# One head's two LRU gates as columns of one weight, rounded parts and remainders stacked along K: two products for three, on one Trainium2 core

## The chip, the core and the metric

The kernel runs on 1 core of one Trainium2 chip. The metric is device time in microseconds (us) of one launch. One core has a TensorE (PE in the profile; PEld is its weight load), a VectorE (DVE), a ScalarE (ACT), a GpSimd (POOL) and a SyncE (SP), which issues the DMAs here. Each takes its instructions in the order in which they were written into its queue.

## The reference

One decoder block over 2048 positions of 1024 channels, in fp32. The part that is changed is the gate of the linear recurrence, `rg_lru`; its 1024 channels are 16 heads of 64, and both gates are block diagonal: one 64x64 matrix per head.

```python
def block_diag_linear(x, w, b):
    xh = x.reshape(bt, s, LRU_HEADS, HEAD_DIM)
    y = jnp.einsum('bshi,hij->bshj', xh, w).reshape(bt, s, LRU_WIDTH)
    return y + b

def rg_lru(x, w_a, b_a, w_x, b_x, lam):
    r = jax.nn.sigmoid(block_diag_linear(x, w_a, b_a))
    i = jax.nn.sigmoid(block_diag_linear(x, w_x, b_x))
    log_a = -LRU_C * r * jax.nn.softplus(-lam)
    a = jnp.exp(log_a)
    bx = jnp.sqrt(-jnp.expm1(2.0 * log_a)) * (i * x)
    # h[t] = a[t] * h[t-1] + bx[t]
```

Around it: RMSNorm, one input projection (columns x and g of the recurrence, c, v and b of a short convolution), a causal convolution of 4 taps on x ahead of the gates, `gelu(g)` behind the recurrence, an output projection, and an MLP with squared ReLU.

## The kernel before

The sequence is cut into four blocks of 512 positions. Channels lie on the 128 partitions, positions along the free dimension. Every fp32 operand of a matmul is split into a part rounded to fp32r ("hi", made by ACT, L153) and a remainder ("lo", made by DVE, L154), and a product is taken as hi·hi + lo·hi + hi·lo (`passes`, L186).

For each block `mixers` (L933) runs four pairs of channel tiles. A pair is 256 channels, two tiles of 128, so four heads. For pair `pr` it runs, in program order, `lru_gelu` (48 matmuls into `ps_g`, then two ACT reads of that PSUM tile: a copy at L566 and a square at L567), `lru_conv` of the next pair (48 matmuls into `ps_x`, ACT copies them to `xr_in` at L536, DVE makes `xr` with 2 instructions at L541 and 6 at L550, then `xr_hi` and `xr_lo`), and `lru_scan` (L572: the gates into two PSUM tiles `psri`, two sigmoids of ACT each at L591 and L592, and then a chain of DVE and ACT instructions up to the scan at L610). After the fourth pair come the units of the short convolution: `ps_c`, `ps_v`, `ps_b`, twice. On PE the stage stands as ps_g, ps_x, psri, ps_g, ps_x, psri, ps_g, ps_x, psri, ps_g, ps_c, psri, ps_v, ps_b, and so on: the matmuls of the gates come one pair late.

PSUM is one pool of four tiles of two banks (L93), taken in turn in program order. In a pair these are ps_g, ps_x, psri, psri, so ps_g of a pair takes the tile of ps_g of the pair before, and the first ps_v takes that of the fourth ps_g. Its first matmul waits until ACT has read that tile for the second time (L567).

The weights of a unit are loaded two units ahead by SP and split by ACT and DVE (L144 to L184), through 15 slots. Temporaries go through 29 slots.

The gate weights are made at the start and again after the first MLP: for each of w_a and w_x a tile of 128 x 8 x 128 is set to zero by POOL (L267), the 64x64 blocks are loaded on its diagonal (L275), and it is split by ACT and POOL (L280). For the eight tiles of channels, both gates and three passes, that makes 6 matmuls per tile of channels and block.

Small parameters are loaded as 88 rows of `prow` (L310), turned by one transpose on PE (L454, `pps`) and copied by DVE to `prm` (L455). PE and DVE run that transpose and copy in the midst of the first projection, which is ordered by hand (L400).

Outside of two hand-ordered parts a planner orders the instructions of each engine's queue by its own estimate of when they can run, so the order on ACT and DVE can differ from block to block. The MLP (L675 to L872) isn't touched.

## Time and profile before

| what | value |
|---|---|
| median of 3 runs | 2218.67 us (2218.43 to 2218.98) |
| the profiled execution's own time | 2218.57 us |
| its span, first to last instruction | 2216.8 us |
| granted TensorE clock, mean of the span | 0.992 |
| PE, PEld busy | 98%, 81% |
| DVE, ACT, POOL busy | 1671.4 us (75%), 1039.1 us (47%), 62.2 us (3%) |
| matmuls, of these psri | 9684, 192 |

Busy time is summed over the span; the stages differ. A row of the timeline gives start, duration, engine, line, operation, output<-input, shapes, count, and in square brackets how long the engine was idle ahead of it and what ended that. The chain of waits follows the end of the program back through what released what; a row of it is start, duration, engine, tile and line.

### The profile page before, as it was taken

The page shows a single profiled execution, that of the slowest core. Times are in us where ns is not written, and L with a number is a line of the kernel's source. Part 1 is how long each engine was busy: PE and PEld are TensorE (multiplying, and loading weights), DVE is VectorE, ACT ScalarE, POOL GpSimd, SP SyncE. Part 2 cuts the span into 40 slices and gives each one's busy share as a digit, 9 for nine tenths or more (in the row PEclk, how much of TensorE's full clock was granted, in tenths as well). Part 3 has the DMA queues.
Part 4 walks back from the last instruction along what each step waited for, and adds up shares of the span by engine and source line. Part 5 has one row for each costly group of instructions (what it writes and reads, how often), then busy time and mean ns, then how long its engine had stood idle before and what let it go on. Part 6 is the DMA issues. An engine that isn't in the chain of part 4 may idle for free.

```text
span 2216.8 us, 25235 instructions
## 1 busy us (share of the span) xinstructions
PE 2176.6 (98%) x9684; PEld 1801.9 (81%) x9684; DVE 1671.4 (75%) x1948; ACT 1039.1 (47%) x1346; POOL 62.2 (3%) x62
## 2 busy tenths in 40 slices
PE   7999999999999999999999999999999999999997
PEld 6888888887888887888888888888888888788886
DVE  7887678868775767878888776886796665887767
ACT  4864478534332333334558644764443332433343
POOL 3010000000000000000100000010000000000000
PEclk8999999999999999999999999999999999999999
DMA  7334443432444386454172434234325345854432
GB/s 226 105 117 152 149 146 119 147 122 86 154 166 148 144 300 248 137 178 151 48 232 91 157 119 171 76 114 147 125 109 185 119 175 203 315 172 161 133 105 76
DMA packets 180776, 334.10 MB, mean 151 GB/s; under 512 B 14672, under 2 KB 106928, under 8 KB 180656
## 3 DMA queue, kind: packets, MB, share of 16 engines
q1 hardware_dynamic: 180656, 332.49, 43.7%
q8 instruction: 76, 1.25, 0.2%
q14 instruction: 44, 0.36, 0.1%
HBM read 252.76 MB, written 79.69 MB: 150 GB/s over the span
## 4 chain that ended last, share of the span: by engine, by line
PE 95%; DVE 4%; SPq 0%; DMA 0%; issue 0%; ACT 0%; DVEq 0%
PE dn L845 27%; PE up L731 26%; PE po L213 11%; PE ps_g L193 8%; PE ps_x L193 7%; PE ps_b L193 4%; PE ps_c L193 4%; PE ps_v L193 4%; PE psri L584 2%; DVE H L154 1%; PE start_x L420 1%; DVE w_lo L154 1%; PE tps L976 1%; DVE x L889 0%; DMA raw<-in_w_in_dram 0%
## 5 line engine op out<-in xcount | busy, mean ns | idle before, releaser
L731 PE MATMUL up<-H,w_hi 128*128 128x512 f32 x1792 | 553.7, 390 | 2.6 <-ACT w_hi L153 1.9
L731 PEld LDWEIGHTS up<-H,w_hi 128*128 128x128 f32 x1792 | 336.6, 188 | 73.5 <-ACT w_hi L153 2.7
L845 PE MATMUL dn<-w_lo,z_hi 128*128 128x512 f32 x896 | 350.2, 391 | 6.7 <-DVE w_lo L154 6.7
L731 PE MATMUL up<-H,w_lo 128*128 128x512 f32 x896 | 349.6, 390 | 3.2 <-DVE w_lo L154 3.2
L845 PE MATMUL dn<-w_hi,z_hi 128*128 128x512 f32 x896 | 349.8, 390 | 0.0
L845 PE MATMUL dn<-w_hi,z_lo 128*128 128x512 f32 x896 | 349.7, 390 | 0.0
L153 ACT CAST w_hi<-w 128x1024 fp32r<-128x1024 f32 x156 | 164.2, 1053 | 345.5 <-PE up L731 169.0
L154 DVE TENSOR_TENSOR w_lo<-w,w_hi 128x1024 fp32r<-128x1024 f32 x156 | 190.5, 1222 | 119.4 <-PE up L731 43.1
L154 DVE TENSOR_TENSOR w_lo<-raw,w_hi 128x1024 fp32r<-128x1024 f32 x156 | 191.6, 1231 | 99.4 <-ACT w_hi L153 45.5
L153 ACT CAST w_hi<-raw 128x1024 fp32r<-128x1024 f32 x160 | 165.6, 1047 | 104.0 <-PE po L213 68.0
L153 ACT CAST z_hi<-z 128x1024 fp32r<-128x1024 f32 x112 | 117.7, 1051 | 199.3 <-PE dn L845 160.9
L845 PEld LDWEIGHTS dn<-w_lo,z_hi 128*128 128x128 f32 x896 | 169.0, 189 | 42.6 <-DVE w_lo L154 7.6
L731 PEld LDWEIGHTS up<-H,w_lo 128*128 128x128 f32 x896 | 168.6, 188 | 39.8 <-DVE w_lo L154 4.9
L845 PEld LDWEIGHTS dn<-w_hi,z_hi 128*128 128x128 f32 x896 | 168.9, 189 | 35.4
L845 PEld LDWEIGHTS dn<-w_hi,z_lo 128*128 128x128 f32 x896 | 169.1, 189 | 35.0
L154 DVE TENSOR_TENSOR z_lo<-z,z_hi 128x1024 fp32r<-128x1024 f32 x112 | 138.3, 1235 | 59.3 <-issue 29.3
L857 DVE TENSOR_TENSOR x<-dn,x 128x1024 f32<-128x1024 f32 x112 | 136.4, 1220 | 23.5 <-PE dn L845 23.4
L213 PE MATMUL po<-w_hi,y_hi 128*128 128x512 f32 x384 | 119.4, 392 | 0.0
L213 PE MATMUL po<-w_hi,y_lo 128*128 128x512 f32 x384 | 118.3, 389 | 0.0
L213 PE MATMUL po<-w_lo,y_hi 128*128 128x512 f32 x384 | 118.3, 389 | 0.0
L193 PE MATMUL ps_g<-h_hi,w_hi 128*128 128x512 f32 x256 | 99.8, 390 | 0.0
L193 PE MATMUL ps_g<-h_lo,w_hi 128*128 128x512 f32 x256 | 99.6, 389 | 0.0
(222 smaller groups left out, 3571.4 us busy)
## 6 DMA issues: line engine op xcount, KB each, us to landing
raw<-in_w_in_dram SPq DMA_DIRECT2D x112, 512.0 KB, 3.6
z<-d_z SPq DMA_DIRECT2D x112, 512.0 KB, 4.2
w<-in_w_mlp_in_dram SPq DMA_DIRECT2D x64, 512.0 KB, 6.1
d_z<-snap SPq DMA_DIRECT2D x64, 512.0 KB, 3.5
raw<-in_w_out_dram SPq DMA_DIRECT2D x48, 512.0 KB, 3.7
d_z<-z SPq DMA_DIRECT2D x48, 512.0 KB, 2.9
w<-in_w_mlp_out_dram SPq DMA_DIRECT2D x48, 512.0 KB, 3.7
x<-in_x_dram SPq DMA_DIRECT2D x20, 512.0 KB, 8.5
```

The lines of the kernel that those rows point to most:

```text
L153: nc.scalar.copy(hi, src)
L154: (lo_engine or V).tensor_tensor(lo, src, hi.bitcast(F32), SUB)
L193: nc.tensor.matmul(ps[:, j, lo:hi], ws[k // 4][:, k % 4, j * P : (j + 1) * P], hs[:, k, lo:hi], start=k == 0 and i == 0, stop=k == KD - 1 ...
L213: nc.tensor.matmul(ps[:, half, :], ys[:, j, t * P : (t + 1) * P], ws[j][:, 0, half * 512 : (half + 1) * 512], start=first and i == 0, stop ...
L420: nc.tensor.matmul(start_x[:, j, 256 * th : 256 * th + 256], w[a][q][:, k, j * P : (j + 1) * P], h[b][:, 4 * q + k, 256 * th : 256 * th + ...
L584: nc.tensor.matmul(pr_[:, half, :], ws[:, c, :], xsrc[:, j, :], start=i == 0, stop=i == len(pl) - 1,)
L731: nc.tensor.matmul(ps[:, j, :], ws[:, k, j * P : (j + 1) * P], hs(k), start=i in (1, 2, 5) and k == 0 and n == 0, stop=k == 3 and n == len ...
L845: nc.tensor.matmul(ps[t // 2][:, t % 2, :], zs[:, p, t * P : (t + 1) * P], ws[:, p, :], start=i in (1, 2, 5) and a == 0 and p == 0 and n == 0,
L857: V.tensor_add(xt[b, th, dh], ps[th], xt[b, th, dh])
L976: nc.tensor.transpose(ps[:, k, :], xs[:, k // 4, k % 4 * P : (k % 4 + 1) * P], ident)
```

## The change

For each head a weight of 128 columns is made: 64 of one gate and 64 of the other, in this order for the even head of a tile (e = 0: w_a, w_x) and the other way round for the odd one (e = 1: w_x, w_a). The 64 rows of the head are loaded twice, on partitions 0 to 63 and 64 to 127. It is split into hi and lo as before, now by ACT and DVE. For each head the moving operand `xr_hl` holds the rounded part of the head's 64 channels on their own partitions (an ACT copy of 64 rows) and the remainder on the other 64 (a DVE subtraction of 64 rows, which writes to other partitions than it reads). The product with the weight's hi sums hi·hi and lo·hi along K, the product with its lo sums hi·lo and lo·lo: two matmuls per head, four per tile of channels. The sigmoids then read 64 rows each: four per tile in place of two, and the x gate is read from the other half of the partitions, for which its bias is loaded once more with the halves swapped (two more DMAs, 96 rows of `prow`). The zeroing by POOL goes; eight DMAs load the weights, not four.

```diff
-    def load_gates(raw):
+    def load_gates():
         res = []
-        for src, r in zip((w_a, w_x), raw):
-            sv = src[0].rearrange("(c e) i j -> e i c j", e=2)
-            for e in range(2):
-                nc.sync.dma_start(
-                    r[64 * e : 64 * e + 64, :, 64 * e : 64 * e + 64], sv[e]
-                )
+        for e in range(2):
+            r = temp("gate_raw", (P, NLRU, P))
+            for g, src in enumerate((w_a, w_x)):
+                col = 64 * ((g + e) % 2)
+                sv = src[0].rearrange("(c e) i j -> e i c j", e=2)
+                for half in range(2):
+                    nc.sync.dma_start(
+                        r[64 * half : 64 * half + 64, :, col : col + 64], sv[e]
+                    )
             hi = temp("gate_hi", (P, NLRU, P), F32R)
             lo = temp("gate_lo", (P, NLRU, P), F32R)
-            split_into(hi, lo, r, nc.gpsimd)
+            split_into(hi, lo, r)
...
     for nm, n in ROWS:
-        nc.sync.dma_start(prow[o : o + n, :], srcs[nm])
+        if nm == "b_x_swapped":
+            for e in range(2):
+                nc.sync.dma_start(
+                    prow[o : o + n, 64 * e : 64 * e + 64],
+                    srcs["b_x"][:, 64 - 64 * e : 128 - 64 * e],
+                )
+        else:
+            nc.sync.dma_start(prow[o : o + n, :], srcs[nm])
...
-        xr_hl = (temp("xr_hi", dt=F32R), temp("xr_lo", dt=F32R))
-        split_into(*xr_hl, xr)
-        return xr, xr_hl
+        xs = []
+        for e in range(2):
+            own, other = slice(64 * e, 64 * e + 64), slice(64 - 64 * e, 128 - 64 * e)
+            st = temp("xr_hl", dt=F32R)
+            nc.scalar.copy(st[own], xr[own])
+            V.tensor_tensor(st[other], xr[own], st[own].bitcast(F32), SUB)
+            xs.append(st)
+        return xr, xs
...
-            for half, wg in enumerate(gates):
-                pl = passes(wg, xr_hl)
-                for i, (ws, xsrc) in enumerate(pl):
+            for e in range(2):
+                for i, wg in enumerate(gates[e]):
                     nc.tensor.matmul(
-                        pr_[:, half, :],
-                        ws[:, c, :],
-                        xsrc[:, j, :],
-                        start=i == 0,
-                        stop=i == len(pl) - 1,
+                        pr_[:, e, :], wg[:, c, :], xr_hl[e][:, j, :], start=i == 0, stop=i == 1
                     )
-            nc.scalar.activation(r[:, j, :], pr_[:, 0, :], AF.Sigmoid, bias=par("b_a", c))
-            nc.scalar.activation(gi[:, j, :], pr_[:, 1, :], AF.Sigmoid, bias=par("b_x", c))
+            for e in range(2):
+                own, other = slice(64 * e, 64 * e + 64), slice(64 - 64 * e, 128 - 64 * e)
+                nc.scalar.activation(
+                    r[own, j, :], pr_[own, e, :], AF.Sigmoid, bias=par("b_a", c)[own]
+                )
+                nc.scalar.activation(
+                    gi[own, j, :], pr_[other, e, :], AF.Sigmoid, bias=par("b_x_swapped", c)[other]
+                )
```

In the order of the instructions three places show what this moves. The first is PE in the second block, at the gates of the fourth pair (second tile of channels) and the first ps_v. Before:

```order
L584 MATMUL psri_2950<-xr_hi_2761,gate_hi_332 128x512
L584 MATMUL psri_2950<-xr_lo_2762,gate_hi_332 128x512
L584 MATMUL psri_2950<-xr_hi_2761,gate_lo_333 128x512
L584 MATMUL psri_2950<-xr_hi_2761,gate_hi_338 128x512
L584 MATMUL psri_2950<-xr_lo_2762,gate_hi_338 128x512
L584 MATMUL psri_2950<-xr_hi_2761,gate_lo_339 128x512
L193 MATMUL ps_v_2998<-h_hi_1570,w_hi_2808 128x512
```

And now, where every helper's line number is a little higher (the kernel grew by some lines):

```order
L593 MATMUL psri_2970<-xr_hl_2779,gate_hi_333 128x512
L593 MATMUL psri_2970<-xr_hl_2779,gate_lo_334 128x512
L593 MATMUL psri_2970<-xr_hl_2782,gate_hi_342 128x512
L593 MATMUL psri_2970<-xr_hl_2782,gate_lo_343 128x512
L194 MATMUL ps_v_3018<-h_hi_1582,w_hi_2828 128x512
```

Two matmuls go per tile of channels, and nothing else on PE changes its place. The second place is ACT in the same pair, from the rounding of the fourth pair's `xr` on; the sigmoids are those of the third pair. Before:

```order
L153 CAST xr_hi_2761<-xr_2752 128x1024
L629 COPY cv_3248<-haloc_392 128x2x2
L591 ACT_TABLE_LOAD
L591 ACTIVATE r_2765<-psri_2767,prm_354 128x512
L592 ACTIVATE gi_2766<-psri_2767,prm_354 128x512
L591 ACTIVATE r_2765<-psri_2776,prm_354 128x512
L592 ACTIVATE gi_2766<-psri_2776,prm_354 128x512
L598 ACTIVATE v_2786<-r_2765,sp4_365 128x512 x2
L602 ACT_TABLE_LOAD
L602 ACTIVATE r_2765<-r_2765,sp8_366 128x512 x2
L566 COPY g_2865<-ps_g_2816 128x1024
L567 ACTIVATE s_2866<-ps_g_2816 128x1024
```

Now the same stretch begins so, and the last two rows come three times more (once for the other head, twice for the other psri tile) ahead of L598's counterpart:

```order
L567 CAST xr_hl_2779<-xr_2770 64x1024
L567 CAST xr_hl_2782<-xr_2770 64x1024
L598 ACT_TABLE_LOAD
L598 ACTIVATE r_2785<-psri_2787,prm_358 64x512
L601 ACTIVATE gi_2786<-psri_2787,prm_358 64x512
```

One cast and four sigmoids more stand ahead of the two reads of the fourth ps_g. The third place is DVE in the first block, around the convolution of the third pair. Before, it stands in one piece (two rows, 8 instructions):

```order
L154 TENSOR_TENSOR w_lo_696<-raw_614,w_hi_695 128x1024
L541 TENSOR_SCALAR xr_752<-xr_in_748,prm_354 128x512 x2
L550 SCALAR_TENSOR_TENSOR xr_752<-xr_in_748,prm_354,xr_752 128x512 x6
L614 SCALAR_TENSOR_TENSOR s_674<-s_674,g_673 128x1024
L154 TENSOR_TENSOR w_lo_809<-raw_687,w_hi_808 128x1024
```

Now its second half reads:

```order
L546 TENSOR_SCALAR xr_760<-xr_in_756,prm_358 128x512
L625 SCALAR_TENSOR_TENSOR s_682<-s_682,g_681 128x1024
L555 SCALAR_TENSOR_TENSOR xr_760<-xr_in_756,prm_358,xr_760 128x512
L155 TENSOR_TENSOR w_lo_819<-raw_695,w_hi_818 128x1024
L555 SCALAR_TENSOR_TENSOR xr_760<-xr_in_756,prm_358,xr_760 128x512
L155 TENSOR_TENSOR w_lo_823<-raw_697,w_hi_822 128x1024
```

The product with g and two remainders of weights have moved in between the instructions that make `xr`. In the other three blocks the convolution of the third pair stays in one piece, and the product with g moves behind it in the second and third.

More of the change, by code (lines that the diff above doesn't have):

```diff
@@ L43 @@
     ("b_x", 8),
+    ("b_x_swapped", 8),
     ("lru_lambda", 8),
@@ L290, in block_kernel @@
     load_xt(0, (1,))
-    gate_raw = gate_tiles()
     load_unit(1)
@@ L448, in block_kernel @@
     with tc.issue_after(last.ins):
-        gates = load_gates(gate_raw)
+        gates = load_gates()
     split_unit(2, nc.gpsimd)
@@ L1172, in block_kernel @@
                     if (i, a) == (7, 0):
-                        gates = load_gates(gate_tiles())
+                        gates = load_gates()
                     if (i, a) == (3, 1):
```

5 lines of the change are left out of this document (removed).

## Prediction

> **What bounds the kernel now.** I read the page's busy shares and chain first, then the chain in order of time, then ACT's and DVE's timelines around the gates. All sums are made against the profiled execution: its time is 2218.57 us, its span 2216.8, so 1.77 us lie around the span; the median of the runs, 2218.67, is 0.1 above it.
>
> ```profile
> PE 2176.6 (98%) x9684; PEld 1801.9 (81%) x9684; DVE 1671.4 (75%) x1948; ACT 1039.1 (47%) x1346; POOL 62.2 (3%) x62
> PE 95%; DVE 4%; SPq 0%; DMA 0%; issue 0%; ACT 0%; DVEq 0%
> ```
>
> PE is busy for 98% of the span and holds 95% of the chain, so time that goes from PE's queue is worth its full length unless another engine then decides. The chain in order of time says where PE never waits. Here are the second block's gates of the first pair and the end of its pairs:
>
> ```profile
> 293.17 2.72 PE psri L584 x12
> 295.89 10.88 PE ps_g L193 x48
> ...
> 355.73 10.88 PE ps_c L193 x48
> 366.61 2.72 PE psri L584 x12
> 369.32 10.88 PE ps_v L193 x48
> ```
>
> Each piece begins where the one before ends: no wait, and 10.88/48 = 0.2267 us per matmul. But a chain without waits doesn't say how near a wait is. ps_v at 369.32 goes into the PSUM tile that the fourth ps_g left, and needs ACT's second read of it. So I look at ACT there: the rounding of the second, third and fourth pair's `xr`, and from the last on what leads to the square that frees the tile:
>
> ```profile
> 299.28 1.06 ACT L153 CAST xr_hi<-xr 128x1024 fp32r<-128x1024 f32 x1 [4.11 <-DVE xr L550]
> ...
> 327.05 1.06 ACT L153 CAST xr_hi<-xr 128x1024 fp32r<-128x1024 f32 x1 [1.65 <-DVE xr L550]
> ...
> 355.89 1.05 ACT L153 CAST xr_hi<-xr 128x1024 fp32r<-128x1024 f32 x1 [5.10 <-DVE xr L550]
> 356.85 0.18 ACT L629 COPY cv<-haloc 128x4 f32<-128x4 f32 x1
> 357.05 1.28 ACT L591 ACT_TABLE_LOAD   x1
> 358.34 0.69 ACT L591 ACTIVATE r<-psri,prm 128x512 f32<-128x512 f32 x1
> 358.93 0.68 ACT L592 ACTIVATE gi<-psri,prm 128x512 f32<-128x512 f32 x1
> 359.50 0.69 ACT L591 ACTIVATE r<-psri,prm 128x512 f32<-128x512 f32 x1
> ...
> 364.54 1.00 ACT L566 COPY g<-ps_g 128x1024 f32<-128x1024 f32 x1
> 365.44 1.02 ACT L567 ACTIVATE s<-ps_g 128x1024 f32<-128x1024 f32 x1
> ```
>
> The square ends at 365.44 + 1.02 = 366.46, and ps_v starts at 369.32. The **lead is 2.86 us**, after a phase on which the recurrence's loop has run at 27.8 and 28.8 us per pair (from cast to cast) and PE at 24.48 (10.88 + 10.88 + 2.72). ACT isn't far from being the bound here although the page has it at 47%; its share in this stage is
>
> ```profile
> 300.00:360.00 60.00, 60.00 (x266) 49.68 (x265) 48.55 (x58) 49.19 (x64) 3.94 (x4) 1.00 0.34 106
> ```
>
> 82% of 60 us. The other blocks have the same place, with these reads and these starts of ps_v:
>
> ```profile
> 131.12 1.03 ACT L567 ACTIVATE s<-ps_g 128x1024 f32<-128x1024 f32 x1
> 1223.29 1.02 ACT L567 ACTIVATE s<-ps_g 128x1024 f32<-128x1024 f32 x1
> 1458.11 1.02 ACT L567 ACTIVATE s<-ps_g 128x1024 f32<-128x1024 f32 x1
> ```
>
> ```profile
> 134.45 10.88 PE ps_v L193 x48
> 1227.12 10.88 PE ps_v L193 x48
> 1461.96 10.88 PE ps_v L193 x48
> ```
>
> Leads of 2.30, 2.81 and 2.83 us: first, third and fourth block.
>
> **The change, part by part.** *Matmuls.* Of 12 in a pair's gates 8 are left: 4 x 0.2267 = 0.907 us per pair, 3.63 per block, 14.5 us for the 64 that go. By this term alone the time is 2204.1.
>
> *ACT.* Per pair one cast and four sigmoids more. Casts of 1024 columns follow each other at 356.85 - 355.89 = 0.96 us, sigmoids of 512 at 359.50 - 358.93 = 0.57. No row shows an ACT or DVE instruction of 64 rows. The upper end is the price at 128 rows, the lower end half of it, if the time went with the rows. The nearest row points to the upper one: the copy at 356.85, 4 columns on all 128 rows, takes 0.18 us against 1.05 for 1024 columns, so it is the columns that set the time. I take the full price: 0.96 + 4 x 0.57 = **3.24 us per pair**. At half price nothing is added at all, since twice as many instructions cost half each.
>
> The Trainium skill, page "ScalarE: Activation LUTs", section "What ACT_TABLE_LOAD costs", gives an activation's time as a constant plus 0.833 ns per element of a lane; by it 64 rows cost what 128 do, and the sum stays as it is. The 0.69 us of the sigmoids above agree with its 0.71 for 512 columns; no run here shows 64 rows.
>
> *DVE.* A second subtraction per pair:
>
> ```profile
> 356.97 1.23 DVE L154 TENSOR_TENSOR xr_lo<-xr,xr_hi 128x1024 fp32r<-128x1024 f32 x1
> 360.80 1.23 DVE L593 TENSOR_TENSOR gi<-gi,xr 128x1024 f32<-128x1024 f32 x1 [2.60 <-ACT gi L592]
> ```
>
> 1.23 us, beside ACT's table load and sigmoids, for which DVE idles 2.60 us anyway. I cost it at nothing; uncovered it would be 1.2 per pair.
>
> *What this does to the loop.* Between the rounding of the second pair's `xr` (299.28, which nothing moves but the same inputs) and the square lie three rounds of casts and sigmoids: 3 x 3.24 = 9.7 us more on ACT. ACT's idle in the stretch doesn't take that up, because it waits there for `xr`, and DVE makes `xr` only after work that waits for ACT's exponentials; the delay goes round. I laid the new order out with the old durations. Second block: the third pair's rounding comes at 328.07 (+1.0; 3.24 minus about 2.2, since the product with g, 1.14, now stands behind the convolution, and the copy to `xr_in` is no longer waited for), the fourth's at 360.5 (+4.6: 3.24 and 0.4 of small statistics), the square ends at +7.8. The third block has the same order: +7.8. The fourth has no statistics of a next block and gets less back: +2.0, +5.0, +8.2. In the first block a product and two remainders move into the third pair's convolution:
>
> ```profile
> 75.62 1.23 DVE L603 SCALAR_TENSOR_TENSOR v<-r,v 128x1024 f32<-128x1024 f32 x1 [2.65 <-ACT r L602]
> ...
> 88.44 4.06 DVE L550 SCALAR_TENSOR_TENSOR xr<-xr_in,prm,xr 128x512 f32<-128x512 f32 x6
> ```
>
> That stretch, 75.62 to 92.50, becomes 20.8 us long, 3.9 more; the square there ends about 12 us later, and the fourth ps_g waits too (some 6 us, which the later wait contains).
>
> PE starts ps_v when the square is done, so each block changes by **delay minus lead**, and the shorter gates only lengthen the wait: 12.0 - 2.3 = 9.7, 7.8 - 2.9 = 4.9, 7.8 - 2.8 = 5.0, 8.2 - 2.8 = 5.4. Together 25.0 us. PE's waits themselves are longer by 3.63 each: some 13 us in all in the first block (6 and 7), 8.5 to 9 in the others. Behind ps_v the short convolution needs less of ACT and the delay isn't paid again.
>
> *Clock.* This program has a place where PE stands still for about 3.6 us:
>
> ```profile
> 1916.00:1920.00 4.00, 0.64 (x3) 0.26 (x2) 3.81 (x4) 2.77 (x4) 0.00 (x0) 0.97 1.03 410
> 1920.00:1924.00 4.00, 4.00 (x12) 3.16 (x13) 4.00 (x4) 1.58 (x2) 0.00 (x0) 0.60 1.03 408
> ```
>
> PE is busy for 0.64 of 4 us, and in the next 4 us the granted clock is 0.60: 3.2 us at half speed, 1.6 to 1.7 us lost. Waits of 7 us and more should each bring that once: 4 x 1.7 = 6.8 us (in the first block the loss after the earlier wait falls into the later one). Ends: 0, and two such stretches per wait, 13.6.
>
> The Trainium skill, page "TensorE: Matmul & The Clock Gate", section "What's actually happening", says that a free-running window of about 3.4 us without work halves the clock until a busy window has passed. By it a wait of over 6.8 us always contains such a window, and what follows costs anything from nothing to one window at half speed and the rest of another. The row at 1920 agrees with one window.
>
> *Start.* PE's transpose of `prow` ends a wait at 23.2:
>
> ```profile
> 15.31 0.35 SPq L310 DMA_DIRECT2D prow<-in_rnn_conv_w_dram  x1
> ...
> 18.12 0.27 SPq L310 DMA_DIRECT2D prow<-in_lru_lambda_dram  x1
> 19.64 0.25 SPq L310 DMA_DIRECT2D prow<-in_g_norm_conv_dram  x1
> 21.24 0.27 SPq L310 DMA_DIRECT2D prow<-in_g_norm_rnn_dram  x1
> ...
> 23.22 0.38 PE L454 MATMUL pps<-ident,prow 88*128 88x88 f32 x1 [1.32 <-DMA prow<-in_g_norm_rnn_dram]
> ```
>
> ```profile
> prow<-in_rnn_conv_w_dram SPq DMA_DIRECT2D x1, 16.0 KB, 6.3
> ```
>
> The issues at 18.12, 19.64 and 21.24 each seem to wait for the landing of the DMA eight places before. Two more stand ahead of the last one now, so it waits for the load issued at 15.31, landed 6.3 us later at 21.6, and leaves at about 21.9: +0.65 us, and PE and DVE with it. Ends: 0, and 3.0 at two more spacings of 1.5.
>
> *Weights of the gates.* POOL's share goes to DVE:
>
> ```profile
> L275 SPq DMA_DIRECT2D gate_raw<-in_w_a_dram x4: 617/627/718, 21.6 to 1058.1; - x4
> L154 POOL TENSOR_TENSOR gate_lo<-gate_raw,gate_hi x4: 2406/2544/3384, 31.4 to 1065.9; 128x1024 fp32r<-128x1024 f32 x4
> ```
>
> ```profile
> 833.77 284.55 PE dn L845 x1247
> ```
>
> Four subtractions of 1.2 us on DVE, two at the start and two at the first MLP's end, where the chain is PE's for 284 us without a break. Four more issues of 0.63 us on SP each time, 2.5 us, ahead of loads that are made two units (21.8 us of PE) before they are used. I cost both at nothing; about 2.5 us each if that cover were gone.
>
> Sum: 25.0 + 6.8 + 0.65 = 32.4 us; 2218.57 + 32.4 = **2251**.
>
> **Rivals.** *The reads aren't late* (not slower). If instructions of 64 rows cost half, ACT has no more to do, the square ends where it did, and each block gains its lead: 2.30 + 2.86 + 2.81 + 2.83 = 10.8 us, less 0.65: 2208.4. For it: PE's share of 98%. Against it: the short copy above. It decides wherever the delay per block is below the lead. 0.09.
>
> *Half the delay is taken up.* ACT idles 5.10 us ahead of the cast at 355.89. If DVE comes earlier there than I laid out, the delay is about 5 us: net 2.1 per block, waits still long enough for the clock: 4 x 2.1 + 6.8 + 0.65 = 15.9, 2234. 0.16.
>
> *The first block's order is the rule.* If the layout is too kind elsewhere, all four lose 9.7: 38.8 + 6.8 + 0.65 = 46, 2265. 0.10.
>
> *The two cancel*: a delay of about the lead in each block, no change. 0.05. That the change doesn't do what it says isn't one: the order shows the 64 matmuls gone.
>
> **How the numbers follow.** The forecast, 2251 (2240 to 2260 by the clock's ends and the start's), has 0.60. The range reaches into the milder case and takes in the harder one: 2227 to 2266, leaving out the gain, no change and the lower part of the milder case. About 0.2% is what a measurement of this kernel can tell from no change. Faster 0.09, same 0.05, slower 0.86.
>
> **What would show it.** Right: in each block PE idle right ahead of the first ps_v for 7 to 9 us with ACT's square of ps_g as what ends it, in the first block also ahead of the fourth ps_g; 8 matmuls in 1.81 us at the gates; sigmoids of 64x512 at 0.69 us; a clock of about 0.5 to 0.6 in the slices behind the waits. Wrong: sigmoids of 64 rows at about 0.4 us, ps_v starting where psri ends, or PE waiting elsewhere (for `xr_hl`, for weights).

## The result and the profile after

The changed kernel takes **2267.82 us** (median of 4 runs, 2267.62 to 2269.32), the one before 2218.55 in the same comparison: 1.0223 times as long, 95% interval 1.0208 to 1.0239. The profiled execution took 2267.62 us, its span is 2265.8, and the mean granted clock 0.980 in place of 0.992. The forecast was 2251 with a range of 2227 to 2266: the direction was right, the loss is 49 us in place of 32.

The page of after: busy time by engine, and the chain's shares.

```profile
PE 2183.7 (96%) x9620; PEld 1800.2 (79%) x9620; DVE 1688.9 (75%) x1968; ACT 1107.1 (49%) x1427; POOL 54.0 (2%) x54
PE 80%; DVE 10%; ACT 7%; issue 2%; SPq 1%; DMA 0%; DVEq 0%; ACTq 0%
```

PE has 64 matmuls less and still holds only 80% of the chain, where it held 95%; DVE and ACT have the rest. PE's waits in after, by tile and by what ended them (us in total, times, longest), say where; before had none of these three:

```profile
PE ps_v L194 <- ACT s L577: 17.7, 4, 4.6
PE ps_g L194 <- ACT s L577: 14.1, 5, 3.8
PE psri L593 <- ACT gi L601: 9.7, 8, 2.4
```

The first is the wait that the prediction named, four times, once per block. The second came in every block, not only in the first. The third wasn't foreseen: the gates' matmuls wait for a PSUM tile from which ACT's sigmoids of the pair before still read. All three wait for ACT, one behind another in the same delay, so that the last one, ahead of ps_v, counts. These are the pieces of the chain in the four blocks, with the square in front of the first:

```profile
147.59 0.93 ACT s L577
...
148.57 13.05 PE ps_v L194 x48
...
393.88 13.28 PE ps_v L194 x48
...
1263.66 13.57 PE ps_v L194 x48
...
1510.14 13.22 PE ps_v L194 x48
```

ps_v starts where the square ends, at 148.57, 393.88, 1263.66 and 1510.14, in place of 134.45, 369.32, 1227.12 and 1461.96. The first is 14.1 us later. With its own 13.05 us in place of 10.88 the next stage starts 16.3 later, so the second block loses 24.56 - 16.28 = 8.28 of its own. In the same way the third block, whose first ps_x starts 27.62 us late, loses 36.54 - 27.62 = 8.92,

```profile
1118.32 10.88 PE ps_x L193 x48
```

```profile
1145.94 4.08 PE ps_x L194 x18
```

and the fourth 48.18 - 39.25 = 8.93 (the shift is told in the same way at its first ps_x). Together 40.2 us, for which the prediction had 25.0 and 0.65 for the start.

Now ACT on the way to the square, at the place that the prediction showed for before (the fourth pair of the second block):

```profile
378.96 2.14 ACT L567 CAST xr_hl<-xr 64x1024 fp32r<-64x1024 f32 x2 [4.80 <-DVE xr L555]
381.11 1.28 ACT L598 ACT_TABLE_LOAD   x1
382.41 0.68 ACT L598 ACTIVATE r<-psri,prm 64x512 f32<-64x512 f32 x1
383.11 0.69 ACT L601 ACTIVATE gi<-psri,prm 64x512 f32<-64x512 f32 x1
383.80 0.69 ACT L598 ACTIVATE r<-psri,prm 64x512 f32<-64x512 f32 x1
...
388.03 1.34 ACT L609 ACTIVATE v<-r,sp 128x512 f32<-128x512 f32 x2
...
392.81 1.02 ACT L577 ACTIVATE s<-ps_g 128x1024 f32<-128x1024 f32 x1
```

One sigmoid of 64 rows takes 0.68 to 0.69 us, as one of 128 rows did; that was forecast. But look at the starts: 382.41, 383.11, 383.80. The next one starts 0.70 later, when the last one is done. Before it started 0.57 later, 0.12 ahead of the end. The two casts take 2.14 together, 1.07 each, where the prediction reckoned with 0.96. From the start of the rounding to the start of the tanh behind the sigmoids before needs 360.64 - 355.89 = 4.75 us, after 388.03 - 378.96 = 9.07. That is 4.32 more, and 4.5 if the small copy is left out (0.19 us, 128x4) that stood in this stretch in before. The prediction had 3.24.

The granted clock behind such a wait (columns as in the prediction's stretches; the clock is the third from the end):

```profile
388.00:392.00 4.00, 1.19 (x4) 0.67 (x4) 1.23 (x1) 3.94 (x7) 0.00 (x0) 0.94 1.01 350
392.00:396.00 4.00, 2.12 (x5) 1.73 (x6) 3.96 (x6) 3.98 (x6) 0.00 (x0) 0.50 0.74 272
396.00:400.00 4.00, 4.00 (x14) 3.13 (x14) 2.66 (x5) 3.96 (x5) 0.00 (x0) 0.70 0.03 10
```

The clock falls while PE still waits, and ps_v runs its first 4.5 us at half speed: from 393.88 to 396 and, by the 0.70, for 2.4 of the last 4 us. Its four pieces last 13.05, 13.28, 13.57 and 13.22 us in place of 10.88: 9.6 us in all, where 6.8 were forecast. (Some 0.6 of it isn't clock: behind a wait the chain draws a piece from its first matmul's start, 0.16 us early.)

### The profile page after: what moved, and what is told of

The parts are those of the page before. It is cut to its first block, busy times and chain, and to the rows that moved or that the text cites. A ratio compares the mean times of both kernels' runs of the same rounds, so it can differ in the third digit from the quotient of the medians.

```text
span 2265.8 us, 25222 instructions
## 1 busy us (share of the span) xinstructions
PE 2183.7 (96%) x9620; PEld 1800.2 (79%) x9620; DVE 1688.9 (75%) x1968; ACT 1107.1 (49%) x1427; POOL 54.0 (2%) x54
## 4 chain that ended last, share of the span: by engine, by line
PE 80%; DVE 10%; ACT 7%; issue 2%; SPq 1%; DMA 0%; DVEq 0%; ACTq 0%
PE dn L856 26%; PE up L742 25%; PE po L214 11%; PE ps_v L194 4%; PE ps_b L194 4%; PE ps_x L194 3%; PE ps_g L194 2%; DVE xr L555 2%; PE ps_c L194 2%; DVE w_lo L155 2%; ACT r L598 1%; ACT gi L601 1%; ACT xr_hl L567 1%; DVE v L621 1%; DVE xr L546 1%
## 5 line engine op out<-in xcount | busy, mean ns | idle before, releaser
L194 PE MATMUL ps_g<-h_hi,w_hi 128*128 128x512 f32 x256 | 104.4, 408 | 14.1 <-ACT s L577 14.1
```

The lines of the kernel that those rows point to most:

```text
L194: nc.tensor.matmul(ps[:, j, lo:hi], ws[k // 4][:, k % 4, j * P : (j + 1) * P], hs[:, k, lo:hi], start=k == 0 and i == 0, stop=k == KD - 1 ...
```

## The experiments

### The same work on ACT with all of PE's matmuls kept

`split64` is the kernel before, with this alone:

```diff
-        split_into(*xr_hl, xr)
+        for e in range(2):
+            own = slice(64 * e, 64 * e + 64)
+            split_into(xr_hl[0][own], xr_hl[1][own], xr[own])
...
-            nc.scalar.activation(r[:, j, :], pr_[:, 0, :], AF.Sigmoid, bias=par("b_a", c))
-            nc.scalar.activation(gi[:, j, :], pr_[:, 1, :], AF.Sigmoid, bias=par("b_x", c))
+            for e in range(2):
+                own = slice(64 * e, 64 * e + 64)
+                nc.scalar.activation(r[own, j, :], pr_[own, 0, :], AF.Sigmoid, bias=par("b_a", c)[own])
+                nc.scalar.activation(gi[own, j, :], pr_[own, 1, :], AF.Sigmoid, bias=par("b_x", c)[own])
```

> The kernel before, with its 12 matmuls per pair kept, and only the cast, the subtraction and the four sigmoids of a pair cut into halves of 64 rows (two casts, two subtractions, eight sigmoids), nothing moved between partitions. Theory A (ACT's added time goes round the loop and alone sets the loss; the four matmuls saved are worth nothing; 64-row instructions follow each other at 0.70 us for a sigmoid and 1.07 for a cast as in the trace of after, so 4.5 us per pair): the first ps_v of a block comes as late as in after, 2262 to 2269 in all, without after's later start and remade gates. Theory B (ACT adds only the 3.24 us per pair of the prediction, and the rest of the loss comes from PE's shorter gates and their order): about 2250. Theory C (time saved or spent on PE's gates counts beside ACT's): 2267.6 + 14.5 = 2282.

`dup128` does each of them twice in full in place of halves:

```diff
         split_into(*xr_hl, xr)
+        split_into(*xr_hl, xr)
...
+            nc.scalar.activation(r[:, j, :], pr_[:, 0, :], AF.Sigmoid, bias=par("b_a", c))
+            nc.scalar.activation(gi[:, j, :], pr_[:, 1, :], AF.Sigmoid, bias=par("b_x", c))
```

> The kernel before with the cast, the subtraction and each of the four sigmoids of a pair done twice in full (128 rows, the second time over the same result): as many instructions as after has, at the pitch of 128 rows (0.57 and 0.96 us, 3.24 per pair). Theory A (the price of after is the missing overlap of 64-row instructions, 1.2 us per pair above 3.24): what the prediction's walk gave, 2245 to 2256, well below the kernel with halves. Theory B (it is the number of instructions, whatever their rows): the same time as the kernel with halves.

Measured: split64 **2260.91** (2258.87 to 2262.94; 1.0193 times before, 1.0178 to 1.0208), dup128 **2255.20** (2254.34 to 2256.52; 1.0168, 1.0151 to 1.0185). Theory A gave 2262 to 2269 and 2245 to 2256, so the first lies 1 us below it and the second inside; B, which wanted 2250 for the first and equal times, and C, 2282, fall. But A's price isn't reached either: it took 4.5 us per pair for any instructions of 64 rows, and split64 costs ACT 4.0. The rows of the sigmoids tell why split64 is cheaper than after. Here the order is r and gi of one half, then of the other:

```profile
377.75 0.69 ACT L595 ACTIVATE r<-psri,prm 64x512 f32<-64x512 f32 x1
378.34 0.67 ACT L596 ACTIVATE gi<-psri,prm 64x512 f32<-64x512 f32 x1
379.02 0.68 ACT L595 ACTIVATE r<-psri,prm 64x512 f32<-64x512 f32 x1
379.61 0.67 ACT L596 ACTIVATE gi<-psri,prm 64x512 f32<-64x512 f32 x1
```

From 377.75 to 378.34 is 0.59, both on the same half; to 379.02 it is 0.68, with a change of halves; then 0.59 again. Nothing in these rows is moved from one half to the other. The stretch from rounding to tanh is 8.55 us here, 7.98 in dup128, 9.07 in after (in before and dup128 the small copy of 0.19 us stands in it, in the other two it doesn't):

| kernel | rounding to tanh, us | delay of the first ps_v, block 1 to 4, us | sum | time, us |
|---|---|---|---|---|
| before | 4.75 | | | 2218.2 |
| dup128 | 7.98 (+3.23) | 9.5, 5.1, 5.2, 5.8 | 25.6 | 2255.2 |
| split64 | 8.55 (+3.80) | 10.5, 7.2, 7.5, 7.7 | 32.9 | 2260.9 |
| after | 9.07 (+4.32) | 14.1, 8.3, 8.9, 8.9 | 40.2 | 2267.8 |

dup128 costs ACT the 3.23 us that the prediction worked out, and its delays are those that the prediction laid out for after, 9.7, 4.9, 5.0 and 5.4. They agree within 0.4 us in every block. So the way from ACT's time to ps_v's delay was right, and the price that went in was not.

### What decides whether two instructions overlap

`pitch` put groups of six equal instructions behind the end of before; `pitch2` did it again with a place of its own for every result. One group, where `A_` is rows 0 to 63 and `B_` 64 to 127:

```diff
+    for n_, (o_, i_) in enumerate([(A_, A_), (B_, B_)] * 3):
+        nc.scalar.activation(q_[n_ // 2][o_, n_ % 2, :], mps[i_, n_ % 2, :], AF.Sigmoid, bias=mb[i_])
```

> The kernel before, with groups of six equal instructions put behind its end, on ACT sigmoids of 512 columns out of PSUM and casts of 1024 columns, on DVE subtractions of 1024 columns, each with 128 rows, with one half of 64 rows, with the halves in turn, and shifted from one half to the other; then copies and products on POOL. The time from start to start is what is read; the total is not compared. Theory A (an instruction of fewer than 128 rows doesn't overlap the next): 0.57 us per sigmoid at 128 rows and 0.70 in every 64-row group. Theory B (instructions overlap unless the next one works on other partitions): 0.57 for one half, 0.70 for the halves in turn. Theory C (only a shift between partitions prevents it): 0.57 for both, 0.70 for the shifted. The casts and subtractions follow the same pattern, 0.96 against 1.07 and 1.13 against 1.24.

> The kernel before, with groups of equal instructions behind its end again, each into places of its own, so that none waits for the one ahead of it to have written; the time from start to start is read and the total is not compared. Sigmoids of 512 columns out of PSUM: 128 rows; one half of 64 rows; the halves in turn; from one half to the other; one half read and both written in turn; both read in turn and one written. Casts (ACT) and subtractions (DVE) of 1024 columns: 128 rows, one half, the halves in turn, and for DVE crossed halves in turn. Theory A (the next instruction starts before the last is done only if it reads and writes the same partitions): 0.58 us for 128 rows, one half, and the plain shift; 0.70 for every group in turn; casts 0.96 for 128 rows and one half, 1.07 in turn; subtractions 1.13 and 1.25. Theory B (only a change of the written partitions counts): 0.58 where both are read and one is written. Theory C (only a change of the read ones): 0.58 where one is read and both are written.

In `pitch` the casts and subtractions wrote over the result of the one ahead and so waited for it (1.07 and 1.25 us from start to start even at 128 rows); only its sigmoids told something, the same as here (its theory B: 0.59 us on one half, 0.70 for the halves in turn). ACT in `pitch2`, each row a group of one kind, its start, and the time from its first start to its last end:

```profile
2214.16 3.00 ACT L1195 ACTIVATE q<-mps,prm 128x512 f32<-128x512 f32 x5
2217.02 3.55 ACT L1198 ACTIVATE q<-mps,prm 64x512 f32<-64x512 f32 x6
2220.44 4.21 ACT L1201 ACTIVATE q<-mps,prm 64x512 f32<-64x512 f32 x6
2224.67 3.55 ACT L1204 ACTIVATE q<-mps,prm 64x512 f32<-64x512 f32 x6
2228.25 4.18 ACT L1207 ACTIVATE q<-mps,prm 64x512 f32<-64x512 f32 x6
2232.46 4.17 ACT L1210 ACTIVATE q<-mps,prm 64x512 f32<-64x512 f32 x6
2236.66 3.88 ACT L1213 CAST qc<-msrc 128x1024 fp32r<-128x1024 f32 x4
2240.45 3.88 ACT L1216 CAST qc<-msrc 64x1024 fp32r<-64x1024 f32 x4
2244.23 4.24 ACT L1219 CAST qc<-msrc 64x1024 fp32r<-64x1024 f32 x4
```

From the start of a group to that of the next, over its count: 128 rows 2.86 / 5 = 0.572 us (L1195), one half 3.42 / 6 = 0.570 (L1198), the halves in turn 4.23 / 6 = 0.705 (L1201), a plain shift from one half to the other 3.58 / 6 = 0.597 with its last one at a change (L1204), one half read and both written in turn 4.21 / 6 = 0.702 (L1207), both read in turn and one written 4.20 / 6 = 0.700 (L1210). Casts: 0.948, 0.945, and 1.06 in turn (4.24 over 4). **Theory A** holds for ACT: an instruction starts ahead of the end of the last only if it reads the partitions that the last one read and writes those that it wrote; 64 rows cost nothing by themselves. B, by which L1210 would overlap, and C, by which L1207 would, fall. The Trainium skill, page "ScalarE: Activation LUTs", section "What ACT_TABLE_LOAD costs", says that ACTIVATEs behind one another overlap by about 93 ns; the rows agree within 30 ns where the partitions stay and show no overlap where they change. DVE's groups were disturbed by waits for places in SBUF and tell nothing on one half; the crossed pair took 2.47 us, 1.25 from start to start, as in after.

In after every one of the eight sigmoids changes either what it reads or what it writes. `sig_order` is after with both tiles' matmuls first and r of one head for both tiles, then its gi, then the other head:

```diff
+        for e in range(2):
+            own, other = slice(64 * e, 64 * e + 64), slice(64 - 64 * e, 128 - 64 * e)
+            for j in range(2):
+                nc.scalar.activation(r[own, j, :], prs[j][own, e, :], AF.Sigmoid, bias=par("b_a", c0 + j)[own])
+            for j in range(2):
+                nc.scalar.activation(gi[own, j, :], prs[j][other, e, :], AF.Sigmoid, bias=par("b_x_swapped", c0 + j)[other])
```

> The kernel after with one thing moved: all eight matmuls of a pair's gates first, then the sigmoids ordered so that two in a row read and write the same partitions (r of one head for both tiles, then gi of that head for both). Three changes of partitions in eight sigmoids in place of seven: 4 x 0.12 = 0.5 us less on ACT per pair. Theory A (ACT's added time alone sets the loss, and each pair's share counts in three rounds per block): 1.5 us per block, 2261 to 2264. Theory B (the first sigmoids now stand behind gates that wait longer for their tiles, since both are let go late): no gain or a loss, 2266 to 2275.

Measured **2263.05** (2262.52 to 2263.36; 1.0198, 1.0181 to 1.0215), 4.8 us less than after: theory A. Its stretch from rounding to tanh is 8.56 us,

```profile
376.76 2.13 ACT L567 CAST xr_hl<-xr 64x1024 fp32r<-64x1024 f32 x2 [4.80 <-DVE xr L555]
...
385.32 1.33 ACT L613 ACTIVATE v<-r,sp 128x512 f32<-128x512 f32 x2
```

the same as split64's 8.55. These two kernels differ in PE's gates, 8 matmuls against 12 per pair, and the one with 8 isn't faster: 2263.05 against 2260.91. So in after's order no worth of the saving on PE can be seen, as the prediction had it ("the shorter gates only lengthen the wait").

### PE's part alone, and the casts alone

`pe_alone` is after with ACT's work of before; `sig_full` puts back only the sigmoids. Both leave out the rearrangement of the halves, so they are for timing alone.

```diff
 # pe_alone
+        xs = [temp("xr_hl", dt=F32R), temp("xr_hl", dt=F32R)]
+        split_into(*xs, xr)
 # both
+            nc.scalar.activation(r[:, j, :], pr_[:, 0, :], AF.Sigmoid, bias=par("b_a", c))
+            nc.scalar.activation(gi[:, j, :], pr_[:, 1, :], AF.Sigmoid, bias=par("b_x", c))
```

> The kernel after with ACT's and DVE's work as before: one cast and one subtraction of 128 rows and four sigmoids of 128 rows over the mixed planes (so the gates are applied to wrong heads: the rearrangement of the halves is left out); the eight matmuls, the new weights and the swapped row stay. Theory A (PE's saving counts until the square of ps_g is late, after a lead of 2.3 to 2.9 us per block, 10.8 in all): 2208, with waits of about 1 us ahead of the first ps_v. Theory B (the square moves forward with PE): the whole 14.5 us, 2204 to 2205. Theory C (something else in the change, its weights, start or order, costs time by itself): above 2212.

> The kernel after with only its eight sigmoids put back to four of 128 rows over the mixed planes (the gates are applied to wrong heads: the rearrangement of the halves is left out); the two casts and the two subtractions of 64 rows stay. It stands between the kernel with PE's part alone (2205) and after. Theory A (the second cast goes round the loop at its 1.17 us, the second subtraction is hidden): three rounds, 3.5 us more per block, less about one of lead that PE's part alone left: 10 us and up to two half-clock stretches, 2213 to 2220. Theory B (the second subtraction, 1.25 us per pair, is on the path too, since the gates' matmuls wait for it): 2222 to 2234.

pe_alone: **2204.97** (2203.61 to 2205.43; 0.9940, 0.9925 to 0.9955). That is 13.2 us below before in the same comparison (2218.18), of 14.5: inside theory B's range. Its matmuls at the first MLP's end last 1.2 us longer than in before, which is clock (shown below, where the prediction is gone through step by step). Its waits show one late square of 1.7 us, in the first block:

```profile
PE ps_v L194 <- ACT s L572: 1.7, 1, 1.7
```

So the square moves forward with PE, and the first rival's 2208 had its step wrong; the new weights, their loads and the swapped row cost nothing that can be seen. sig_full: **2227.04** (2223.60 to 2227.74; 1.0037, 1.0023 to 1.0051), 22 us above pe_alone for 1.17 us per pair, inside theory B's number. But the second subtraction isn't the cause. In sig_full the two of the fourth pair of the second block run from 365.95 to 368.42, and then DVE idles until ACT's sigmoids are done:

```profile
369.58 1.23 DVE L598 TENSOR_TENSOR gi<-gi,xr 128x1024 f32<-128x1024 f32 x1 [1.16 <-ACT gi L597]
```

With one subtraction it would idle longer and start no earlier. It waits so in 12 of the 16 pairs. The first ps_v is 8.0, 2.0, 2.7 and 2.8 us later than in pe_alone (each without the shift that the block began with), 15.5 together, which is A's mechanism, though more than its 10; and all five waits for the square, of 2.0 to 3.6 us, brought a stretch at half speed, 1.7 to 2.7 us lost each, where A had reckoned with two. So theory B's number came out by luck. This is the second block's wait of 1.97 us:

```profile
375.30 0.50 PE L194 MATMUL ps_v<-h_hi,w_hi 128*128 128x512 f32 x1 [1.97 <-ACT s L577]
```

```profile
374.00:376.00 2.00, 0.70 (x3) 0.62 (x4) 2.00 (x4) 2.00 (x3) 0.00 (x0) 1.00 0.96 344
376.00:378.00 2.00, 2.00 (x8) 1.60 (x7) 2.00 (x3) 1.97 (x4) 0.00 (x0) 0.69 1.05 387
378.00:380.00 2.00, 2.00 (x6) 1.53 (x5) 2.00 (x6) 2.00 (x3) 0.00 (x0) 0.50 1.02 386
380.00:382.00 2.00, 2.00 (x9) 1.61 (x9) 2.00 (x3) 1.97 (x3) 0.00 (x0) 0.96 0.03 9
```

The clock is 1.00 through the wait and 0.69, 0.50 and 0.96 in the stretches behind it: about 3.4 us at half speed, 1.7 lost, where after's waits of 3.8 to 4.6 us ahead of ps_v lost 2.0 to 2.5. The wait of 1.7 us in pe_alone was followed by none (granted 1.00 from 128 to 140 us).

### Taking work off ACT

`wcast_sq_pool` gives POOL the rounding of the mixers' column weights and the square; `all_relief` adds one head's rounding of `xr` (the last lines) and the order of `sig_order`.

```diff
-        nc.scalar.copy(hi, src)
+        nc.gpsimd.tensor_copy(hi, src)
...
-        nc.scalar.activation(s, psg, AF.Square)
+        nc.gpsimd.tensor_tensor(s, g, g, MUL)
...
-            nc.scalar.copy(st[own], xr[own])
+            (nc.gpsimd.tensor_copy if e else nc.scalar.copy)(st[own], xr[own])
```

> The kernel after with work taken from ACT to POOL, which idles: the rounding of the mixers' column weights (three casts of 1.0 us per pair) and the square of g, made from the copy in SBUF, so that the tile that ps_v needs is free when ACT's copy of it is done, 0.9 us earlier. Theory A (the sum of ACT's work per pair decides): 3.1 + 0.9 us less per pair, near what before had, 2206 to 2216. Theory B (only what stands between the rounding of xr and the read of ps_g counts; of the three casts about one does, the others fill waits): about 0.9 + 3 x 1.0 us less delay per block, 2245 to 2255. Theory C (POOL's work slows DVE beside it): 2255 or more, with DVE's instructions longer than their 1.22 us.

> The kernel with ACT's work on POOL, and besides the second head's rounding of xr on POOL, beside ACT's first, and the sigmoids in the order with three changes of partitions: another 1.07 + 0.5 us less on ACT per pair, both between the rounding of xr and the read of ps_g. Theory A: PE alone decides, 2204 to 2210, faster than both kernels. Theory B (of the two moved blocks of work only part counts): 4.7 us less delay per block than the kernel with ACT's work on POOL alone, by its number 2226 to 2240. Theory C (DVE slowed by POOL): no faster than that kernel.

Measured **2286.99** (1.0307, 1.0292 to 1.0322) and **2273.01** (1.0244, 1.0229 to 1.0259): the first slower than after by 19 us, which is theory C; the second 14 us below the first, so C falls for it, and 33 us above B's range, so none of the three holds. The groups from 60 to 140 us of wcast_sq_pool (mean ns behind the busy time):

```profile
L158 DVE TENSOR_TENSOR w_lo<-raw,w_hi 128x1024 fp32r<-128x1024 f32 x15 | 23.6, 1590 | 0.1
L155 POOL CAST w_hi<-raw 128x1024 fp32r<-128x1024 f32 x13 | 20.9, 1625 | 24.7 <-DVE w_lo L158 14.2 <-PE ps_g L197 7.5 <-issue 1.8
```

With nothing beside it, POOL casts such a tile in 1.04 us (`pitch`):

```profile
L1227 POOL CAST mh<-msrc 128x1024 fp32r<-128x1024 f32 x4 | 4.1, 1036 | 780.8 <-DVE ml L1225 780.8
```

Beside DVE it takes 1.63, and DVE's subtraction 1.59 in place of 1.22. The loop runs over ACT and DVE, so what ACT gets back DVE loses; that this is the whole of the 19 us isn't shown. The Trainium skill, page "GPSIMD Engine Reference", section "Key points", says that GpSimd shares its SBUF interfaces with VectorE; these rows agree.

### Giving PE other work for the time that it waits

In after the loop of ACT and DVE lasts 30.0 and 33.4 us per pair (from cast to cast, second block). If PE has 23.6 for it, PE could do pieces of the short convolution there. Here are the orders of PE's pieces in a block, from ps_g of the first pair on: g, x, c, v and b are ps_g to ps_b of 10.88 us each, G a pair's gates, S the recurrence's statistics.

```
after            g x G g x G g x G g c G v b c v S b
inter_after      g x G g c x G g v x G g b c G v b S
one_moved        g x G g c x G g x G g v G b c v b S
one_moved_late   g x G g x G g c x G g v G b c v b S
two_moved        g x G g x G g c x G g v b G c v b S
two_moved_early  g x G g c x G g x G g v b G c v b S
```

In code, for one_moved_late (the list of units is put in the same order):

```diff
+            if pr == 2:
+                gc = conv_c(0, h)
-            nx = lru_conv(pr + 1, h) if pr < 3 else conv_c(0, h)
+            nx = lru_conv(pr + 1, h) if pr < 3 else conv_v(0, h, gc)
...
-        u = conv_v(0, h, xr)
-        ysA[0], accA = conv_b(0, h, accA, u)
+        ysA[0], accA = conv_b(0, h, accA, xr)
...
-        rB = stats(accB, D, "B")
         ysA[1], accA = conv_b(1, h, accA, u)
+        rB = stats(accB, D, "B")
```

`inter_before` and `one_moved_before` are the same orders on before, `inter_order` and `one_moved_order` add the sigmoids' order of sig_order.

> The kernel after, with the order of PE's pieces changed: the first convolution pair's three pieces (ps_c, ps_v, ps_b of 10.88 us each), which stood behind the four recurrence pairs, now stand one each in the second, third and fourth of them. ACT's and DVE's work is the same. PE's share of such a pair becomes 10.88 x 3 + 1.81 = 34.5 us, more than the recurrence's loop takes in after (30 to 33 us). Theory A (after loses only because PE has less to do per pair than the loop takes, so that ACT's read of ps_g comes late): the waits for ACT's square vanish and PE's saving counts, 2204 to 2212, faster than both kernels. Theory B (the loop's time has to be paid somewhere, now behind the last pair, where less of PE's work is left to cover its end): waits at the statistics or the output rows, 2215 to 2240.

> The kernel before with the same new order of PE's pieces and nothing else. PE has no wait in the mixers there, so theory A: no gain, 2214 to 2222. Theory B (the new order is worth something by itself, apart from the change): 2205 to 2212, as fast as the new order with the change.

> The new order of PE's pieces on after, with the sigmoids in the order with three changes of partitions in place of seven as well (0.5 us less on ACT per pair). Theory A (ACT is off the path once PE has enough to do): within 2 us of the new order alone. Theory B (ACT still counts): 4 to 6 us less than that, as much as it was worth in after's own order (4.7 us).

Measured: inter_after **2278.10** (1.0271, 1.0257 to 1.0285), above both theories, with B's mechanism; inter_before 2236.22 (1.0079, 1.0066 to 1.0092), which neither theory had: this order costs before 18 us; inter_order 2269.30 (1.0234, 1.0218 to 1.0250), 8.8 us less than inter_after, so ACT still counts: theory B, with more than its 4 to 6. In inter_after no matmul waits for the square any more, and this took its place:

```profile
PE sps L519 <- DVE v L516: 38.3, 4, 18.7
```

The statistics need the last pair, and only 21.8 us of PE's work (v and b) are left to cover the end of its chain; in before, PE waits there too then, 9.1 us in all. So one piece alone was moved, which leaves 43.5 us there:

> The kernel after with one piece of PE moved: ps_c of the first convolution pair, 10.88 us, stands in the second recurrence pair (behind its ps_g) in place of the fourth; ps_v comes where ps_c was. The work behind the last pair, ahead of the statistics, stays 43.5 us long. Theory A (the delay, 8.3 to 9 us per block and more in the first, is covered by a piece that PE has ready in time): the waits for the square nearly vanish, 2204 to 2215, faster than both kernels. Theory B (the time goes to the statistics or to ps_v's own inputs instead): 2225 or more, with PE waiting there.

> The same with the sigmoids in the order with three changes of partitions: 0.5 us less on ACT per pair. Theory A: no wait is left to shorten, within 2 us of the kernel with one piece moved, 2203 to 2213. Theory B (ACT still sets the end of these stages): 3 to 5 us less than it.

> As the kernel with one piece moved, but ps_c stands in the third recurrence pair. Theory A (the piece can come any time ahead of the first wait of that length): the same within 3 us, a little more where in the first block the third ps_g already waited. Theory B (only a piece that lies ahead of most of the delay covers it): 5 us or more slower than the early place.

> The kernel before with the same one piece moved to the second pair. PE has no wait in its mixers, so theory A: no change, 2215 to 2222. Theory B (the order changes what ACT and DVE do and costs time by itself): 2225 or more, as three pieces moved cost before 18 us.

Measured: one_moved 2247.04 (1.0131, 1.0116 to 1.0147), with the other order of sigmoids 2248.60 (1.0136, 1.0122 to 1.0149), **one_moved_late 2236.63** (1.0082, 1.0069 to 1.0094), one_moved_before 2218.48 (0.9999, 0.9990 to 1.0008). The early order is worth nothing on before and 21 us on after, so much of the loss was a matter of what PE had ready. The late one gains 31 us on after; on before it wasn't run. The loss doesn't all go. In one_moved_late ps_g and ps_v no longer wait for the square, and the next piece that takes the tile does:

```profile
PE ps_b L191 <- ACT s L574: 11.2, 3, 4.3
```

The late place is 10 us better than the early one, which neither theory had: with the piece early, PE waits at the gates again (psri 11.5 us in one_moved, 1.5 in one_moved_late). For one_moved theory B's number holds, though PE doesn't wait where it said (the statistics, ps_v's inputs) but at the gates, ps_c and ps_b; for one_moved_before theory A holds; the other order of sigmoids gained nothing on one_moved, though not for A's reason, since waits were left: it lets go of the tiles of the gates later, and the second ps_c waits 16.9 us for them. The last two moved ps_b as well:

> The kernel after with two pieces of PE moved ahead of the fourth gates: ps_c of the first convolution pair in the third recurrence pair, as in the late place, and ps_b behind ps_v, ahead of the fourth gates in place of behind them. Behind the last gates 32.6 us of PE's work are left ahead of the statistics. Theory A (the second piece covers what was left): the wait for the square and the half-clock stretches behind it go, 11 + 7 us less than the late place, 2210 to 2222. Theory B (the last pair's chain, some 31 to 40 us, then ends behind PE's work): waits at the statistics of several us in each block, 2225 to 2245.

> The same with ps_c in the second recurrence pair, as in the early place. Theory A: the place of ps_c matters little once two pieces are moved, within 4 us of the other. Theory B (as with one piece, where the late place was 10 us faster): 5 to 12 us slower than the other.

2249.20 (1.0144, 1.0128 to 1.0159) and 2250.85 (1.0146, 1.0129 to 1.0163): slower than one piece in the late place; for the first theory B, 4 us above its range, for the second theory A, so the place of ps_c matters little here. The wait moved on to the second ps_c and the statistics:

```profile
PE ps_c L191 <- ACT gi L598: 18.9, 3, 7.5
PE sps L519 <- DVE v L516: 7.1, 1, 7.1
```

No order that was tried beats before. Whether one exists stays open.

## Why the prediction was wrong, step by step

- *Matmuls.* 64 gone, 14.5 us: right, as pe_alone shows (13.2 us). That they are worth nothing here: right.
- *ACT.* **This step failed in its size.** "I take the full price: 0.96 + 4 x 0.57 = 3.24 us per pair" measured 4.5. The durations were right (0.68 and 1.05 us at 64 rows). The 0.57 and 0.96 were times from start to start, read off instructions that all work on the same 128 partitions, and were given to instructions that change partitions each time and don't overlap: 8 x 0.70 for the sigmoids, where 8 x 0.57 was reckoned, and 2 x 1.07 for the casts. It had also been called the upper end, which it wasn't. That 64 rows cost the full duration was right, but the row that it was read from couldn't show it: the copy of 4 columns and the cast of 1024 both have 128 rows. Three rounds of 1.25 us per block and four blocks are 15 us; the delays came out 40.2 - 25.0 = 15.2 us above the forecast.
- *Delay minus lead.* Right as a rule: dup128, whose ACT costs the forecast's 3.23, has 25.6 us of delays where 25.0 were laid out. After lost 8.3 to 8.9 where 4.9 to 5.4 stood, and 14.1 for 9.7, with the place, ACT's square ahead of the first ps_v, as forecast. Wrong in part: ahead of ps_v PE waits 3.8 to 4.6 us and not 7 to 9, since the fourth ps_g waits in every block and the gates wait too; both waits lie inside the delay.
- *Clock.* Forecast 6.8, measured 9.6 behind the four waits, within the ends of 0 and 13.6. At two places outside the mixers, behind a wait that both kernels have, the clock went other ways. Near the end before ran 3.2 us at half speed, and after keeps its full clock behind the same wait of 3.36 us: the matmuls behind it last 269.40 us, 1.58 less than in before (270.98).

```profile
1970.28 269.40 PE dn L856 x1187
```

- *DVE's second subtraction.* Hidden, as forecast: sig_full's row shows it, and dup128, which has it too, has the delays laid out.
- *Start.* Forecast +0.65 us; the transpose runs 0.36 us earlier than in before (23.22). The last load of `prow` is issued at 21.13, not at 21.9, and in before at 21.24.

```profile
22.86 0.39 PE L459 MATMUL pps<-ident,prow 96*128 96x96 f32 x1 [1.18 <-DMA prow<-in_g_norm_rnn_dram]
```

- *Weights of the gates.* Costed at nothing, and no cost can be seen. The matmuls at the first MLP's end take 285.62 us in place of 284.55, but in dup128, which has before's weights, they take 285.77. It is the clock behind a wait of 3.4 us again. Here are after, dup128, and then the 6 us behind that wait in before and in after:

```profile
860.32 285.62 PE dn L856 x1247
852.01 285.77 PE dn L848 x1247
```

```profile
833.40:839.40 6.00, 5.63 (x18) 4.47 (x19) 4.86 (x5) 0.00 (x0) 0.00 (x0) 0.72 1.03 394
860.00:866.00 6.00, 5.68 (x13) 4.46 (x14) 4.81 (x5) 0.00 (x0) 0.00 (x0) 0.50 1.02 399
```

Sum: 40.2 for the delays, 9.6 for the clock behind them, and -1.6 and +1.1 for the clock at the two other places, 49.3 us against the span's 49.0. Of the 16.6 us above the forecast of 32.4, the delays make 15.2, by ACT's price; the clock makes 2.3 more, and the start 0.65 less. Of the rivals, "the first block's order is the rule" came nearest in time, 2265, but not by what happened: the blocks lost 8.3 to 8.9, not 9.7 each, and the first lost 14.1.

## What to carry to other kernels

Read from a timeline both the duration of an instruction and the time to the next start, and ask what the overlap hangs on before giving it to other instructions. An engine that is busy for 47% of the span can stand in a loop with another and decide a stage: here 4.5 us more of ACT per pair cost 49 us in all, where the saving on PE (14.5 us) counts only as long as PE doesn't wait for that loop. Order instructions on part of the partitions so that neighbours read and write the same ones: here that gained 4.8 us, though nothing with one piece of PE moved, where the tiles of the gates were let go later.

## What the runs showed of the hardware that was not expected

- ACT starts an instruction about 0.12 us ahead of the end of the last only where it reads and writes the same partitions as that one: sigmoids of 512 columns every 0.570 us on one half, 0.705 on the halves in turn; casts 0.945 and 1.06.
- How long PE waits doesn't tell what the clock costs: a wait of 1.97 us was followed by about 3.4 us at half clock (1.7 us lost), one of 1.7 us by none, and waits of 3.4 us at the MLPs' ends cost 1.7 us (before, 833), 2.8 (after, 860) and nothing (after, 1970). The Trainium skill, page "TensorE: Matmul & The Clock Gate", section "What's actually happening", puts the half clock behind an idle window of about 3.4 us; the wait of 1.97 us disagrees.
- POOL and DVE slow each other: casts of 1.04 us alone take 1.63 to 1.78, subtractions of 1.22 take 1.40 to 1.59 (all_relief and wcast_sq_pool, from 60 to 140 us).
